# A hybrid decoder trunk: the low halves off the diagonal given to GpSimd, and the mask of the maxima added within VectorE's maximum

## The chip, the cores and the metric

The kernel runs on one core of a Trainium2 chip. The metric is the device time of one execution in microseconds (us). The core has five engines that take their instructions in order, each from its own queue: TensorE (PE, matrix products into PSUM banks), VectorE (DVE), ScalarE (ACT), GpSimd (POOL) and SyncE (SP, which issues most DMAs).

## The reference, cut to what matters

A sequence of 2048 tokens passes a Mamba-2 mixer and then a layer of multi-head latent attention with 16 heads; the change is in the attention alone. Its core is

```
for i in range(S // Q_BLOCK):
    q0 = i * Q_BLOCK
    kv_len = q0 + Q_BLOCK
    s = einsum('bqhd,bkhd->bhqk', q_nope[:, q0:kv_len], k_nope[:, :kv_len]) + \
        einsum('bqhr,bkr->bhqk', q_rope[:, q0:kv_len], k_rope[:, :kv_len])
    mask = (q0 + local)[:, None] >= arange(kv_len)[None, :]
    p = softmax(where(mask, s * scale, -inf))
    outs.append(einsum('bhqk,bkhd->bqhd', p, v[:, :kv_len]))
```

A query and a key have 96 elements in a head (64 and 32 rotary ones), a value 64. The results are wanted close to float32, so the kernel holds operands as pairs of float16 numbers, a high half and a low half, and multiplies the pairs.

## The kernel before, in words

The layers before the attention take about the first 2000 us of the program, the attention the next 800, and the output projection with the last norm (`back`) the rest. In the attention a **job** is one head with one quarter of the queries (512, four blocks of 128): 64 jobs, head by head, quarter by quarter. Each job does two things.

**Maxima** (`maxima`, L1224). For each block of 128 queries, TensorE forms the scores against all its keys with queries on the partitions, high halves only (L1236), in chunks of at most 1024 keys, one or two a block. Where a chunk ends on the diagonal, a further product adds the 128x128 mask (L1238). VectorE takes the maximum of each row of the chunk (L1239). When the last chunk of a job is done, some small VectorE instructions make the four columns of maxima into two float16 rows: `m` (L1244, where blocks had two chunks), `me` (L1248), the cast into `nm` (L1250), its low half (L1251), and a transpose `rT` (L1253). SyncE writes `rT` to HBM (L1254) and reads it back as rows 96 and 97 of the job's queries (L1257), so that the score product subtracts the maximum by itself.

**Scores and values.** The keys of a job are taken two blocks at a time, a **duo**. `scores` (L1260) forms the transposed scores, keys on the partitions, by three products for each block (L1269 to L1271) and a mask on the diagonal (L1273). ScalarE takes the exponential into `x` (L1276) and its high half into `PTs` (L1278). The **low** half, `x` less the high half, is two instructions: the first 512 columns on VectorE (L1279), the rest on GpSimd (L1280). Off the diagonal a duo has 1024 columns; the two on the diagonal have 896 and 384. `values` (L1283) then multiplies each 128 columns with V by three products (L1296 to L1298), the third with the low half. `finish` (L1305) divides the sums (L1310, L1313, tiles `ri` and `Op`), and for every second head `store` (L1318) transposes two heads' results.

The order on TensorE is written out by hand (L1342 to L1357): at each **step** first the chunks of maxima that are due (at most 1024 columns a step, at latest four steps ahead of the job's first duo), then a waiting store, then the scores of one duo, then the values of the duo that came HELD steps before. The other engines' order is the scheduler's, fixed when the program is built. The PSUM banks `s` are three for chunks, scores and stores together, so TensorE waits until VectorE or ScalarE has read an earlier one.

A head has 20 steps. They are counted here from 0 in each head: steps 0 and 1 are the first quarter (both on the diagonal), 2 to 5 the second, 6 to 11 the third, 12 to 19 the fourth; the last two of each quarter are on the diagonal. The maxima of the fourth quarter end with a 1024 chunk at step 8, and its first scores are at step 12. Chunk, maximum, scores, values and low are named by the step or duo, as in "low 7".

Of the kernel before, what the change touches and what calls it, by code (L numbers as in the profile page):

```python
# [37 lines left out]
SZ = 4  # L38
EV0 = ['big', 'Xp', 'big', 'Sp', 'wsp']
EV1 = ['big', 'yT', 'Xp', 'big', 'Sp']  # L40
HELD = 2
READY = 4
TURN = 2
MSCALE = 64.0
# [22 lines left out]
class Net:  # L67
# [1124 lines left out]
    def heads(self, sp):  # L1192
# [3 lines left out]
        for u in turned:  # L1196
            nc.gpsimd.memset(u, 0.0)

        def cuts(kv):

            first = kv if kv <= 2 * TB else TB if kv <= 3 * TB else 2 * TB
            return [(0, first)] + ([(first, kv - first)] if kv > first else [])
# [21 lines left out]
        def maxima(n, j, i, c0, w, last):  # L1224

            h, qb = jobs[n]
            if (j, i) == (0, 0):
                peak[n] = self.t(sp, "mx", [P, 4, 2], bufs=3)
                if n + 2 < len(jobs):
                    self.load_q(*jobs[n + 2])  # L1230
            Q, K, qs = quer[h, qb], keys[h % 2], slice(j * P, (j + 1) * P)
            s = bank().rearrange("p a b -> p (a b)")
            for at in range(0, w, TB):
                c = min(TB, w - at)
                diag = last and at + c == w
                mm(s[:, at:at + c], Q[0:96, 0, qs], K[0:96, 0, c0 + at:c0 + at + c], start=True, stop=not diag)  # L1236
                if diag:
                    mm(s[:, w - P:w], self.idb, self.mk, start=False, stop=True)  # L1238
            v.tensor_reduce(peak[n][:, j, i:i + 1], s[:, :w], AX.X, ALU.max)  # L1239
            if last and j == 3:  # L1240
                m = peak.pop(n)
                if i:
                    x = self.t(sp, "m", [P, 4], bufs=2)
                    v.tensor_tensor(x, m[:, :, 0], m[:, :, 1], ALU.max)  # L1244
                else:
                    x = m[:, :, 0]
                e = self.t(sp, "me", [P, 4], bufs=2)
                v.tensor_scalar(e, x, -1.0 / MSCALE, LN16 / MSCALE, ALU.mult, ALU.add)  # L1248
                u = turned[n % 2]
                v.tensor_copy(u[:, 0:4], e)  # L1250
                v.tensor_tensor(u[:, 4:8], e, u[:, 0:4], ALU.subtract)  # L1251
                r = self.t(sp, "rT", [P, 32], F16, bufs=2)
                v.transpose(r, u)  # L1253
                nc.sync.dma_start(self.m_d[n], r)  # L1254
                rows = self.m_d[n].rearrange("(g r) q -> r g q", r=32)
                for k in range(2):
                    nc.sync.dma_start(quer[h, qb][96 + k:97 + k, 0, :].rearrange("p (j g q) -> p j g q", j=4, q=32),  # L1257
                                      rows[4 * k:4 * k + 4].unsqueeze(0))

        def scores(n, kb):  # L1260

            h, qb = jobs[n]
            Q, K, s = quer[h, qb], keys[h % 2], bank()
            ja, jb = max(kb - 4 * qb, 0), max(kb + 1 - 4 * qb, 0)
            at, end = ja * P, 2 * TB - jb * P
            for b, j in enumerate((ja, jb)):
                ks, c = slice((kb + b) * P, (kb + b + 1) * P), slice(j * P, TB)
                o = s[:, 1, 0:TB - j * P] if b else s[:, 0, c]
                mm(o, K[0:98, 0, ks], Q[0:98, 0, c], start=True, stop=False)  # L1269
                mm(o, K[0:96, 0, ks], Q[0:96, 1, c], start=False, stop=False)  # L1270
                mm(o, K[0:96, 1, ks], Q[0:96, 0, c], start=False, stop=kb < 4 * qb)  # L1271
                if kb >= 4 * qb:
                    mm(o[:, 0:P], self.mk, self.idb, start=False, stop=True)  # L1273
            s = s.rearrange("p a b -> p (a b)")[:, at:end]
            x = self.t(sp, "x", [P, 2 * TB], bufs=3)
            act(x[:, at:end], s, AF.Exp)  # L1276
            u = self.t(sp, "PTs", [P, 2, 2 * TB], F16, bufs=HELD + 2)
            act(u[:, 0, at:end], x[:, at:end], AF.Copy)  # L1278
            v.tensor_tensor(u[:, 1, at:TB], x[:, at:TB], u[:, 0, at:TB], ALU.subtract)  # L1279
            nc.gpsimd.tensor_tensor(u[:, 1, TB:end], x[:, TB:end], u[:, 0, TB:end], ALU.subtract)  # L1280
            return u

        def values(n, kb, u):  # L1283

# [44 lines left out]
                with self.tc.issue_after(done.ins):  # L1329
                    self.load_wo(qb)  # L1330

        step, later, held, made = [0], [], [], 0
        self.load_k(1, 0, NB)
        self.load_v(1)

        def waiting():
            for at, f in list(later):
                if at <= step[0]:
                    later.remove((at, f))
                    f()  # L1340

        for i, (n, kb) in enumerate(duos):  # L1342
            step[0] = i
            while cols[made] < due[i]:
                maxima(*chunks[made])
                made += 1
            waiting()
            held.append((n, kb, scores(n, kb)))
            if len(held) > HELD:
                values(*held.pop(0))  # L1350
        while held:
            step[0] += 1
            values(*held.pop(0))
            waiting()
# [201 lines left out]
```

## Time and profile before

| | us |
|---|---|
| median of 3 runs | 2988.53 (2984.73 to 2989.96) |
| the profiled execution, its own time | 2990.72 |
| its span in the profile | 2988.5 |
| TensorE busy in the span | 2869.4 (96%) |
| VectorE busy | 2255.6 (75%) |
| ScalarE busy | 1795.1 (60%) |
| GpSimd busy | 807.5 (27%) |

The profile is one execution as the hardware profiler recorded it, with starts counted from the span's start. L12 is a line of the kernel. A row of a group gives line, engine, operation, the tiles it writes and reads, shapes and count, then the busy time, the mean of one in ns, and the idle time of the engine just before with what ended it. In a timeline a row gives start and length in us. In the list of waits a row gives who waited for whom, with us in total, times and the longest. Records of TensorE overlap, since a product starts while the one before it drains.

### The profile page before, as it was taken

How to read it: one execution, taken by the hardware profiler on the slowest of the kernel's cores; microseconds unless marked ns; L12 is line 12 of the kernel's file. 1: busy time of each engine (PE TensorE's matmuls, PEld its weight loads, DVE VectorE, ACT ScalarE, POOL GpSimd, SP SyncE). 2: the span in 40 equal slices, each digit the busy share in tenths (PEclk: the TensorE clock that was granted, in tenths of full speed). 3: DMA queues.
4: the chain of work that ended last, by engine and by line, in shares of the span. 5: the costliest groups of instructions: out<-in, count | busy, mean ns of one | idle time of the engine just before them, and what ended most of it. 6: DMA issues, size and time to landing. Idle time of an engine off the chain costs nothing.

```text
span 2988.5 us, 58345 instructions
## 1 busy us (share of the span) xinstructions
PE 2869.4 (96%) x21838; PEld 1689.2 (57%) x21838; DVE 2255.6 (75%) x4570; ACT 1795.1 (60%) x3592; POOL 807.5 (27%) x862
## 2 busy tenths in 40 slices
PE   7899999999999999999999999999999999998998
PEld 3456556555555554554554554546666666665787
DVE  6789987787877878788766435358989999989454
ACT  8777656665766656556553433327777777777422
POOL 0212122121221212222212112215454445455300
PEclk9999999999999999999999999999999999999999
DMA  8765435544464446545447655641222121222452
GB/s 286 242 216 176 165 122 194 172 155 141 154 228 158 139 169 201 186 157 191 136 130 249 197 171 177 193 154 44 54 57 65 49 62 46 70 65 75 151 203 106
DMA packets 244751, 441.28 MB, mean 148 GB/s; under 512 B 69842, under 2 KB 111506, under 8 KB 243028
## 3 DMA queue, kind: packets, MB, share of 16 engines
q1 hardware_dynamic: 233332, 401.64, 42.0%
q0 software_dynamic: 11136, 35.92, 3.3%
q8 instruction: 171, 2.80, 0.4%
q14 instruction: 112, 0.92, 0.1%
HBM read 332.73 MB, written 104.73 MB: 146 GB/s over the span
## 4 chain that ended last, share of the span: by engine, by line
PE 33%; DVE 10%; ACT 5%; issue 3%; DMA 1%; POOL 1%; SPq 0%; DVEq 0%; ACTq 0%; POOLq 0%
DVE PTs L1279 4%; PE mm L83 4%; PE mm L84 4%; PE mm L85 4%; DVE mx L1239 3%; PE tr L83 3%; PE tr L84 3%; PE tr L85 3%; PE s L1269 2%; PE s L1270 2%; PE s L1271 2%; ACT x L1276 2%; ACT PTs L1278 2%; PE s L1236 2%; PE o L1298 1%
## 5 line engine op out<-in xcount | busy, mean ns | idle before, releaser
L1280 POOL TENSOR_TENSOR PTs<-x,PTs 128x512 f16<-128x512 f32 (+1 forms) x320 | 381.0, 1193 | 397.4 <-ACT PTs L1278 195.0
L1276 ACT ACTIVATE x<-s 128x1024 f32<-128x1024 f32 (+1 forms) x320 | 285.1, 891 | 190.3 <-PE s L1271 105.0
L1239 DVE TENSOR_REDUCE mx<-s 128x1 f32<-128x1024 f32 (+7 forms) x384 | 339.5, 900 | 30.7 <-PE s L1238 19.3
L1279 DVE TENSOR_TENSOR PTs<-x,PTs 128x512 f16<-128x512 f32 x320 | 291.5, 922 | 46.0 <-ACT PTs L1278 21.2
L83 PE MATMUL mm<-xT,wsp 128*128 128x512 f16 x800 | 306.5, 383 | 8.1 <-ACT wsp L114 6.3
L84 PE MATMUL mm<-xT,wsp 128*128 128x512 f16 x800 | 305.8, 382 | 0.0
L85 PE MATMUL mm<-xT,wsp 128*128 128x512 f16 x800 | 304.8, 381 | 0.0
L1278 ACT ACTIVATE PTs<-x 128x1024 f16<-128x1024 f32 (+1 forms) x320 | 296.9, 928 | 9.9
L1269 PE MATMUL s<-xT,K 98*128 98x512 f16 (+3 forms) x640 | 223.3, 349 | 25.7 <-DVE mx L1239 17.7
L1298 PE MATMUL o<-K,PTs 128*128 128x65 f16 x2176 | 235.2, 193 | 11.4 <-DVE PTs L1279 7.2
L1297 PE MATMUL o<-K,PTs 128*128 128x65 f16 x2176 | 236.3, 194 | 0.0
L1296 PE MATMUL o<-K,PTs 128*128 128x64 f16 x2176 | 236.0, 192 | 0.0
L83 PE MATMUL mm<-wsp,xT 128*128 128x512 f16 (+1 forms) x640 | 231.1, 362 | 3.9 <-ACT craw L605 3.7
L84 PE MATMUL mm<-wsp,xT 128*128 128x512 f16 (+1 forms) x640 | 231.2, 362 | 3.2 <-DVE wsp L115 3.2
L611 DVE SCALAR_TENSOR_TENSOR cacc<-craw,pack,cacc 128x512 f32<-128x512 f32 x288 | 214.6, 773 | 24.0 <-ACT cacc L609 23.0
L85 PE MATMUL mm<-wsp,xT 128*128 128x512 f16 (+1 forms) x640 | 231.1, 361 | 0.0
L801 POOL TENSOR_TENSOR Xp<-Xw,Xp 128x512 fp32r<-128x512 f32 x64 | 89.5, 1399 | 501.0 <-ACT Xp L800 301.2
L1270 PE MATMUL s<-xT,K 96*128 96x512 f16 (+3 forms) x640 | 223.7, 350 | 0.0
L1271 PE MATMUL s<-xT,K 96*128 96x512 f16 (+3 forms) x640 | 222.4, 348 | 0.0
L1296 PEld LDWEIGHTS <-PTs 128*128 128x128 f16 x2176 | 203.1, 97 | 27.5 <-issue 0.4
L1297 PEld LDWEIGHTS <-PTs 128*128 128x128 f16 x2176 | 201.6, 97 | 23.1 <-issue 0.3
L1298 PEld LDWEIGHTS <-PTs 128*128 128x128 f16 x2176 | 200.5, 98 | 15.3 <-DVE PTs L1279 8.5
(459 smaller groups left out, 7178.2 us busy)
## 6 DMA issues: line engine op xcount, KB each, us to landing
wsp<-wi_d SPq DMA_DIRECT2D x96, 512.0 KB
big<-cumT SPq DMA_DIRECT2D x64, 512.0 KB
wraw<-in_ssm_w_out_dram SPq DMA_DIRECT2D x96, 256.0 KB
wi_d<-wsp SPq DMA_DIRECT2D x32, 512.0 KB
wsp<-wo_d SPq DMA_DIRECT2D x32, 512.0 KB
wsp<-wu_d SPq DMA_DIRECT2D x28, 512.0 KB
hx<-in_ssm_w_in_dram SPq DMA_DIRECT2D x48, 256.0 KB
wraw<-in_ssm_w_in_dram SPq DMA_DIRECT2D x48, 256.0 KB
```

Of the source, the lines that this page charges most:

```text
L83: mm(out, l_hi, r_hi, start=start, stop=False)
L84: mm(out, l_hi, r_lo, start=False, stop=False)
L85: mm(out, l_lo, r_hi, start=False, stop=stop)
L1239: v.tensor_reduce(peak[n][:, j, i:i + 1], s[:, :w], AX.X, ALU.max)
L1270: mm(o, K[0:96, 0, ks], Q[0:96, 1, c], start=False, stop=False)
L1276: act(x[:, at:end], s, AF.Exp)
L1278: act(u[:, 0, at:end], x[:, at:end], AF.Copy)
L1279: v.tensor_tensor(u[:, 1, at:TB], x[:, at:TB], u[:, 0, at:TB], ALU.subtract)
L1280: nc.gpsimd.tensor_tensor(u[:, 1, TB:end], x[:, TB:end], u[:, 0, TB:end], ALU.subtract)
L1296: mm(o[:, 0:64], hi, V[:, k, 0:64], start=k == 0 and j == 0, stop=False, skip_group_check=True)
L1297: mm(o[:, 0:65], hi, V[:, k, 64:129], start=False, stop=False, skip_group_check=True)
L1298: mm(o[:, 0:65], lo, V[:, k, 64:129], start=False, stop=k == 4 * qb + j, skip_group_check=True)
```

## The change

The diff, with unchanged lines left out:

```
-HELD = 2
+HELD = 3
...
+        fence = self.t(sp, "fence", [P, 2 * TB], BF16, bufs=1)
+        nc.gpsimd.memset(fence[:, :2 * TB - P], 0.0)
+        nc.gpsimd.tensor_copy(fence[:, 2 * TB - P:], self.mk)
...
             for at in range(0, w, TB):
                 c = min(TB, w - at)
-                diag = last and at + c == w
-                mm(s[:, at:at + c], Q[0:96, 0, qs], K[0:96, 0, c0 + at:c0 + at + c], start=True, stop=not diag)
-                if diag:
-                    mm(s[:, w - P:w], self.idb, self.mk, start=False, stop=True)
-            v.tensor_reduce(peak[n][:, j, i:i + 1], s[:, :w], AX.X, ALU.max)
+                mm(s[:, at:at + c], Q[0:96, 0, qs], K[0:96, 0, c0 + at:c0 + at + c], start=True, stop=True)
+            if last:
+                junk = self.t(sp, "junk", [P, 2 * TB], BF16, bufs=1)
+                v.tensor_tensor_reduce(junk[:, :w], s[:, :w], fence[:, 2 * TB - w:], 1.0, -3.0e38, ALU.add, ALU.max,
+                                       accum_out=peak[n][:, j, i:i + 1])
+            else:
+                v.tensor_reduce(peak[n][:, j, i:i + 1], s[:, :w], AX.X, ALU.max)
...
-            v.tensor_tensor(u[:, 1, at:TB], x[:, at:TB], u[:, 0, at:TB], ALU.subtract)
-            nc.gpsimd.tensor_tensor(u[:, 1, TB:end], x[:, TB:end], u[:, 0, TB:end], ALU.subtract)
+            if kb < 4 * qb:
+                lows(u, x, at, end, nc.gpsimd)
+            else:
+                fresh.append((u, x, at, end, v))
             return u
+
+        def lows(u, x, at, end, engine):
+
+            engine.tensor_tensor(u[:, 1, at:end], x[:, at:end], u[:, 0, at:end], ALU.subtract)
...
             waiting()
+            if fresh:
+                lows(*fresh.pop())
             held.append((n, kb, scores(n, kb)))
             if len(held) > HELD:
                 values(*held.pop(0))
+        lows(*fresh.pop())
```

Four things happen. The low half of a duo off the diagonal is one GpSimd instruction of 1024 columns (192 of them) instead of two of 512 on two engines. The low half of a duo on the diagonal is one VectorE instruction of 896 or 384 columns (64 of each), written in the program one step later, behind that step's maxima. The 256 maxima whose chunk ends on the diagonal add a row of zeros and the mask, the tile `fence`, within the instruction that takes the maximum; each is two VectorE instructions, the sum with the maximum and the reading of the accumulator, and 256 mask products of TensorE go. And values follow three steps behind the scores instead of two.

The changed lines move the scheduler's order on VectorE. The first place is steps 8 to 12 of the ninth head: the maxima `mx` of steps 7 and 8, the small instructions that end the fourth quarter's maxima (`m` to `rT`), and the lows (`PTs<-x`). Before, from the maximum of step 8 to the one behind low 11:

```order
L1239 TENSOR_REDUCE mx_28854<-s_29128 128x1
L1279 TENSOR_TENSOR PTs_29111<-x_29109,PTs_29111 128x512
L1244 TENSOR_TENSOR m_29133<-mx_28854 128x4
L1248 TENSOR_SCALAR me_29135<-m_29133 128x4
L1250 CAST nm_4004_21664<-me_29135 128x4
L1251 TENSOR_TENSOR nm_4004_21664<-me_29135,nm_4004_21664 128x4
L1253 STREAM_TRANSPOSE rT_29139<-nm_4004_21664 128x32
L1279 TENSOR_TENSOR PTs_29153<-x_29151,PTs_29153 128x512
L1279 TENSOR_TENSOR PTs_29191<-x_29189,PTs_29191 128x512
L1279 TENSOR_TENSOR PTs_29230<-x_29228,PTs_29230 128x512
L1239 TENSOR_REDUCE mx_29297<-s_29302 128x1
L1279 TENSOR_TENSOR PTs_29269<-x_29267,PTs_29269 128x256
```

And now, from the same maximum to low 11; L1242 is the masked maximum with its reading, L1250 to L1259 are `m` to `rT`, L1322 and L1325 a finish, L1293 a low:

```order
L1242 ISA junk_28953,mx_28674<-s_28950,fence_21667 128x1024
L1242 ISA mx_28674 128x1
L1250 TENSOR_TENSOR m_28955<-mx_28674 128x4
L1254 TENSOR_SCALAR me_28957<-m_28955 128x4
L1256 CAST nm_4004_21664<-me_28957 128x4
L1322 RECIPROCAL ri_28987<-o_28846 128x4
L1257 TENSOR_TENSOR nm_4004_21664<-me_28957,nm_4004_21664 128x4
L1325 TENSOR_TENSOR Op_28989<-o_28846,ri_28987 128x4x64
L1259 STREAM_TRANSPOSE rT_28961<-nm_4004_21664 128x32
L1293 TENSOR_TENSOR PTs_29039<-x_29037,PTs_29039 128x896
L1242 ISA junk_29110,mx_29103<-s_29108,fence_21667 128x128
L1293 TENSOR_TENSOR PTs_29077<-x_29075,PTs_29077 128x384
```

Low 7 no longer stands ahead of `m`, nor lows 8 and 9 behind `rT`; a finish has come in between the cast and the transpose; lows 10 and 11 stand around the first maximum of step 12 as they did, longer than before. (The reading behind L1242 of step 12 lies between the last two rows.)

The second place is steps 0 to 2 of the same head on VectorE, from the last maximum of step 0, which ends the third quarter's maxima. Before:

```order
L1239 TENSOR_REDUCE mx_28618<-s_28802 128x1
L1244 TENSOR_TENSOR m_28807<-mx_28618 128x4
L1248 TENSOR_SCALAR me_28809<-m_28807 128x4
L1250 CAST nm_4003_21663<-me_28809 128x4
L1251 TENSOR_TENSOR nm_4003_21663<-me_28809,nm_4003_21663 128x4
L1253 STREAM_TRANSPOSE rT_28813<-nm_4003_21663 128x32
L1239 TENSOR_REDUCE mx_28854<-s_28859 128x1
L1279 TENSOR_TENSOR PTs_28829<-x_28827,PTs_28829 128x512
L1279 TENSOR_TENSOR PTs_28874<-x_28872,PTs_28874 128x256
L1310 RECIPROCAL ri_28887<-o_28534 128x4
L1239 TENSOR_REDUCE mx_28854<-s_28893 128x1
```

And now:

```order
L1242 ISA junk_28623,mx_28433<-s_28620,fence_21667 128x1024
L1242 ISA mx_28433 128x1
L1293 TENSOR_TENSOR PTs_28591<-x_28589,PTs_28591 128x384
L1250 TENSOR_TENSOR m_28625<-mx_28433 128x4
L1254 TENSOR_SCALAR me_28627<-m_28625 128x4
L1256 CAST nm_4003_21663<-me_28627 128x4
L1257 TENSOR_TENSOR nm_4003_21663<-me_28627,nm_4003_21663 128x4
L1245 TENSOR_REDUCE mx_28674<-s_28679 128x1
L1259 STREAM_TRANSPOSE rT_28631<-nm_4003_21663 128x32
L1293 TENSOR_TENSOR PTs_28648<-x_28646,PTs_28648 128x896
L1242 ISA junk_28721,mx_28674<-s_28718,fence_21667 128x640
```

The low of the last diagonal duo (384) now stands behind the last maximum of step 0 and not ahead of the step; the low of step 0's duo (896) stands ahead of the maximum of step 2 as before, and that of step 1's duo has moved behind it.

More of the change, by code (lines that the diff above doesn't have):

```diff
@@ L1330, in store @@
                     self.load_wo(qb)
-        step, later, held, made = [0], [], [], 0
+        step, later, held, fresh, made = [0], [], [], [], 0
         self.load_k(1, 0, NB)
```

## The prediction, made before the changed kernel was run

> **What bounds the kernel now.** I read the page first, then the busy time by stretches, the waits, the groups by shape, and one head of the attention in order of time. The change touches only the attention, so the stretches come first; a row gives its length, then busy time and instructions of TensorE, its weight loads, VectorE, ScalarE and GpSimd.
>
> ```profile
> 2200.00:2400.00 200.00, 190.88 (x2536) 126.12 (x2535) 182.22 (x288) 152.44 (x175) 98.68 (x85) 1.00 0.22 55
> 2400.00:2600.00 200.00, 190.11 (x2513) 125.14 (x2512) 182.94 (x294) 150.39 (x173) 96.90 (x83) 1.00 0.23 60
> ```
>
> TensorE shows 95% busy, VectorE 91%, ScalarE 76%, GpSimd 49%, at the full granted clock (1.00). Busy time overstates TensorE, because records overlap. How far apart its products start, and how long a head lasts, stands in the timeline (start, length, idle before in brackets):
>
> ```profile
> 2380.31 0.38 PE L1269 MATMUL s<-xT,K 98*128 98x512 f16 x1 [0.72 <-DVE mx L1239]
> 2419.28 0.38 PE L1269 MATMUL s<-xT,K 98*128 98x512 f16 x1
> 2419.50 0.38 PE L1270 MATMUL s<-xT,K 96*128 96x512 f16 x1
> 2425.78 0.19 PE L1296 MATMUL o<-K,PTs 128*128 128x64 f16 x1
> 2425.87 0.19 PE L1296 MATMUL o<-K,PTs 128*128 128x64 f16 x1
> 2426.57 0.22 PE L1238 MATMUL s<-mk,idb 128*128 128x128 bf16 x1
> 2426.63 0.27 PE L1236 MATMUL s<-K,xT 96*128 96x256 f16 x1
> 2427.39 0.22 PE L1238 MATMUL s<-mk,idb 128*128 128x128 bf16 x1
> 2428.69 0.38 PE L1269 MATMUL s<-xT,K 98*128 98x512 f16 x1 [1.08 <-DMA xT<-m_d]
> 2443.13 0.22 PE L1238 MATMUL s<-mk,idb 128*128 128x128 bf16 x1
> 2444.30 0.38 PE L1236 MATMUL s<-K,xT 96*128 96x512 f16 x1 [0.95 <-DVE mx L1239]
> ```
>
> A 512-column product takes 0.217 us of the queue, three small value products 0.09, a mask 0.06. A head has 17408 columns of scores (34 times 512), so 102 x 0.217 = 22.1 us of scores, 7.4 of maxima, 408 x 0.03 = 12.2 of values, 32 x 0.06 = 1.9 of masks, 0.4 of transposes: 44 us. From step 12 of one head (2380.31) to the next (2428.69) are 48.4. So TensorE waits 4.3 us a head, and an idle row hides 0.16 more (0.38 of record less 0.217). Two of the waits are above, at steps 12 and 17: 1.3 and 1.2 us between starts, less the 0.06. What TensorE waits for:
>
> ```profile
> PE s L1269 <- DVE mx L1239: 17.7, 35, 1.7
> PE s L1236 <- DVE mx L1239: 7.2, 10, 1.0
> PE o L1298 <- DVE PTs L1279: 7.2, 11, 2.3
> ```
>
> So TensorE bounds the attention, and VectorE being late with the maxima, whose banks must come free, is what it waits for.
>
> **The change, part by part.**
>
> *Masks of the maxima.* 256 products of 0.06 us go: 0.96 us a head. Seven of the sixteen stand just ahead of the two waits below (steps 0, 2, 8 and the four of 12); there TensorE only waits longer. Nine count: -0.5 us a head.
>
> *Masked maximum.* The groups of VectorE, with mean ns of one:
>
> ```profile
> L1279 DVE TENSOR_TENSOR PTs<-x,PTs 128x512 f16<-128x512 f32 x256 | 250.5, 979 | 44.2 <-ACT PTs L1278 20.5 <-POOL PTs L1280 17.3 <-PE o L1298 5.7
> L1239 DVE TENSOR_REDUCE mx<-s 128x1 f32<-128x1024 f32 x111 | 134.3, 1210 | 6.9 <-PE s L1236 5.6 <-PE s L1238 0.3
> L1239 DVE TENSOR_REDUCE mx<-s 128x1 f32<-128x512 f32 x77 | 51.9, 673 | 4.7 <-PE s L1236 4.6
> L1313 DVE TENSOR_TENSOR Op<-o,ri 128x256 f32<-128x256 f32 x64 | 26.9, 421 | 1.6
> L1239 DVE TENSOR_REDUCE mx<-s 128x1 f32<-128x256 f32 x15 | 6.2, 411 | 0.0
> L884 ACT ACTIVATION_READ_ACCUMULATOR yt<-y 128x1 f32 x64 | 12.0, 187 | 0.0
> ```
>
> No such sum with a maximum runs before. Its nearest row is L1313, one input in PSUM and one in SBUF: 421 ns for 256, against 411 for the plain maximum, so the main part costs the same. It issues a second instruction that reads the accumulator: from 0 (hidden in the overlap of neighbours) to 187 ns (ScalarE's row). I take 0.1, as VectorE's rows overlap by about that. In all 26 us, inside the stretches below.
>
> *Low halves.* VectorE's 256 lows of 512 and 64 of 256 leave; 64 of 896 and 64 of 384 come. At 1.05 ns an element ((1210 - 673) / 512) and from an undisturbed 0.69 for 512, they take 1.09 and 0.56: 106 us. GpSimd's time comes from its undisturbed rows, and what it does to VectorE from the stretch around the maximum of step 8, now:
>
> ```profile
> 2403.55 0.91 POOL L1280 TENSOR_TENSOR PTs<-x,PTs 128x384 f16<-128x384 f32 x1 [2.74 <-DVE nm L1250]
> 2422.43 1.16 POOL L1280 TENSOR_TENSOR PTs<-x,PTs 128x512 f16<-128x512 f32 x1 [0.40 <-ACT PTs L1278]
> 2420.35 1.67 POOL L1280 TENSOR_TENSOR PTs<-x,PTs 128x512 f16<-128x512 f32 x1 [0.70 <-DVE mx L1239]
> 2402.86 0.16 DVE L1244 TENSOR_TENSOR m<-mx 128x4 f32<-128x4 f32 x1
> 2419.11 1.21 DVE L1239 TENSOR_REDUCE mx<-s 128x1 f32<-128x1024 f32 x1
> 2420.32 0.69 DVE L1279 TENSOR_TENSOR PTs<-x,PTs 128x512 f16<-128x512 f32 x1
> 2420.93 1.11 DVE L1244 TENSOR_TENSOR m<-mx 128x4 f32<-128x4 f32 x1
> 2422.08 0.17 DVE L1248 TENSOR_SCALAR me<-m 128x4 f32<-128x4 f32 x1
> 2422.49 1.11 DVE L1251 TENSOR_TENSOR nm<-me,nm 128x4 f16<-128x4 f32 x1
> 2423.64 0.21 DVE L1253 STREAM_TRANSPOSE rT<-nm 128x32 f16<-128x32 f16 x1
> ```
>
> (1.16 - 0.91) / 128 is 1.95 ns an element, so 1024 take 2.16 us; 192 of them are 415 us of some 785, and GpSimd is not the bound. But m and nm, four elements wide, take 1.11 us where GpSimd is at work and 0.16 where not: a VectorE instruction with two inputs in SBUF waits until GpSimd's has ended. GpSimd's are now twice as long.
>
> The Trainium skill speaks against this part: "GPSIMD Engine Reference", Engine selection, puts two-input elementwise work on VectorE, GpSimd being about twice as slow. The rows say 1.16 against 0.69 (1.7 times); twice VectorE's 1.23 for 1024 would be an estimate of 2.5, which would add 0.3 to each blocked instruction below.
>
> *Entry.* The first maximum now needs the fence, which GpSimd writes last:
>
> ```profile
> 1999.47 0.28 DVE L1239 TENSOR_REDUCE mx<-s 128x1 f32<-128x128 f32 x1
> 1999.85 0.68 POOL L1103 DMA_DIRECT2D qn_d<-Xp  x1 [1.27 <-DVE mx L1239]
> 2000.41 0.31 POOL L1197 MEMSET nm<- 128x32 f16 x2
> ```
>
> GpSimd is free at 2000.7; a memset of 896 and a copy of 128 cost between 0.3 (two like the memsets here) and 1.8 us (896 elements at the two-input rate). I take 0.8, near the middle: the maximum starts at 2001.5, +2 us, once; queued behind it are all later maxima, and the first scores wait for them.
>
> *Step 17 and step 11.* No VectorE low is left between the maxima there: the wait at 2444.30 goes, -1.1 us a head. The maximum of step 16 now stands behind nm of step 15, which GpSimd may hold up for most of 2 us: +0.3.
>
> *Steps 0 to 3.* From the maximum of step -1 to the one of step 2 VectorE now does 896, 512, 1024 and 1024, 640 of maxima, and lows of 1.09, 0.56, 1.09 with m to rT (0.9) between: 1.09 + 0.67 + 1.21 + 1.21 + 0.81 + 2.74 + 0.9 + 0.3 (reads) = 8.9 us, in one piece. TensorE needs from that chunk to the scores of step 3, by the spacings above, 3.8 for scores, 2.4 for values and 1.8 for chunks: 8.0. Scores 3 take the bank of step 2's chunk, so they wait 0.9 to 1.2, and two ScalarE waits behind them may add 0.3. Now it waits in these steps, the second only in heads that store:
>
> ```profile
> 2402.88 0.27 PE L1269 MATMUL s<-xT,K 98*128 98x256 f16 x1 [0.37 <-DVE mx L1239]
> 2407.43 0.41 PE L1323 MATMUL s<-pack,Op 128*128 128x128 f32 x2 [0.60 <-DVE Op L1313]
> ```
>
> With 0.16 hidden in each, 0.5 to 1.3, and I take +0.2.
>
> *Steps 8 to 12, which decide.* With HELD 3 TensorE does the values of duo 4 (21 products, 0.63 us) ahead of chunk 8, not those of duo 5 (0.27), so chunk, maximum and scores of step 8 come 0.37 later against duo 7, less the mask's 0.06. Low 7 stays where it is on GpSimd, 2420.35. Maximum 8 ends at 2420.45, just behind, so m waits to 2420.35 + 2.16 = 2422.5 (now 2422.04). me, the cast and the reciprocal of a finish that now stands ahead of nm bring nm to 2423.1; low 8 has started at 2422.43 + 0.37 = 2422.8 and holds it to 2424.96. Then Op (0.42, now ahead of the transpose) and rT: 2425.6, against 2423.85. From there the row's way through HBM takes 2428.69 - 2423.85 = 4.84 us, so the scores of step 12 start at 2430.4, not at 2428.69 as here, where the row came last, nor near 2428.35, as in heads where VectorE's maxima did (the row at 2380.31): +1.7 to +2.05. What VectorE does itself meets it there:
>
> ```profile
> 2425.17 0.95 ACT L1278 ACTIVATE PTs<-x 128x896 f16<-128x896 f32 x1
> 2427.87 1.47 DVE L1239 TENSOR_REDUCE mx<-s 128x1 f32<-128x256 f32 x3
> ```
>
> Low 10 waits for this copy (2426.5 then) and for GpSimd's low 9 (to 2427.1); low 10, a 128 maximum, low 11 and the 256 maximum, whose bank scores 12 takes, need 1.09 + 0.4 + 0.56 + 0.5: 2429.65, against 2427.87 + 0.41 = 2428.3 now. So +1.3 even if m slipped in first. I take +2.0.
>
> *Sum.* -0.5 - 1.1 + 0.3 + 0.2 + 2.0 = +0.9 us a head; some 15 heads are in this rhythm: +13, and +2 at the entry. The profiled execution took 2990.7 (span 2988.5), so 3006; the median of the runs shown lies 2.2 lower: 3003.
>
> **The rivals.**
>
> *Relief.* VectorE has 190 lows fewer, and TensorE's waits are for VectorE. If low 7 starts after m, and lows 10 and 11 are done when chunk 12 comes, the waits at 12 and 17 go (1.1 each) and all masks count: 16 x (2.2 + 0.96) = 51, less the entry's 2 and the 0.2 and 0.3 a head: about 2948. For it: GpSimd's start beats m by 0.1 us only. Against it: low 10 and low 9 by the rows above.
>
> *The stretches cancel.* m slips in first, lows 10 and 11 do not: -0.5 - 1.1 + 0.5 + 1.3 = +0.2 a head, +3, and the entry: 2994, no change that can be told.
>
> *A dear masked maximum.* Each 0.3 us longer (from 0.1 on it costs; half the rate would be 0.5 to 1): three stand in steps 0 to 3 and three in the way to scores 12, 6 x 0.3 x 16 = +29 on the forecast, 3032. It would also do so by waiting for GpSimd. Against it: L1313 keeps 421 ns. [...]
>
> **How the numbers follow.** A measurement of this kernel tells some 0.2% (6 us) from no change. Forecast 0.46, since m's 0.1 us and the order of lows 10 and 11 are two separate reasons; relief 0.24; cancelling 0.20; dear maximum 0.10. Slower is 0.56, same 0.20, faster 0.24. The range leaves out the lower half of relief and the upper half of the dear maximum: 2948 to 3035. The forecast's own range is 2995 to 3015 (m and low 10 between their ends).
>
> **What would show it.** Right: L1238 gone; GpSimd's lows at 2.1 to 2.3 us; m and nm at step 8 held for 2 us each; scores 12 idle 2 to 4 us in every head, by the row or by VectorE; no wait at step 17; head period 49.3. Wrong: the masked maximum of 1024 above 1.4 us with its read, m at 0.16 in step 8, or a head period under 48.

## The result, and the profile after

| | before | changed |
|---|---|---|
| median, us | 2986.89 (4 runs, 2984.73 to 2989.96) | 3110.91 (4 runs, 3107.97 to 3113.17) |
| the profiled execution, us | 2990.72 | 3112.48 |
| its span, us | 2988.5 | 3110.7 |

The ratio is 1.0414, 95% interval 1.0396 to 1.0432. The change costs 124 us where 16 were forecast. The first scores of the attention start at 2009.45 us (2009.66 before), and 195 us lie behind its last scores (196 before), so all of it lies inside the attention. The busy time by stretches of the changed kernel, with the columns of the prediction's rows (length, then TensorE, its weight loads, VectorE, ScalarE and GpSimd, the granted clock of TensorE, the DMA share, GB/s):

```profile
2200.00:2400.00 200.00, 171.06 (x2064) 108.01 (x2061) 145.77 (x261) 129.75 (x147) 93.24 (x44) 0.90 0.17 44
2400.00:2600.00 200.00, 177.71 (x2163) 113.63 (x2162) 147.49 (x262) 133.64 (x154) 89.32 (x43) 0.90 0.21 54
```

VectorE fell from 182 busy of 200 to 146, for the most part because the same work is spread over longer heads: with the lengths of a head below, it is busy for 44 us of a head before and for 41 now. TensorE fell from 190 to 174, and the granted clock from 1.00 to 0.90. No engine is full, so look for waits. This is VectorE's timeline in the eighth head, from the end of the maximum of step 8 to the transpose, then GpSimd's lows at the same time, then TensorE (start, length, engine and line, idle before in brackets):

```profile
2423.37 1.23 DVE L1242 CUSTOM_DVE_ANT_0 junk<-s,fence 128x1024 bf16<-128x1024 f32 x1 [1.15 <-PE s L1239]
2424.64 2.05 DVE L1250 TENSOR_TENSOR m<-mx 128x4 f32<-128x4 f32 x1
2426.72 0.17 DVE L1254 TENSOR_SCALAR me<-m 128x4 f32<-128x4 f32 x1
2426.93 2.14 DVE L1256 CAST nm<-me 128x4 f16<-128x4 f32 x1
2429.10 2.04 DVE L1257 TENSOR_TENSOR nm<-me,nm 128x4 f16<-128x4 f32 x1
2431.06 0.41 DVE L1325 TENSOR_TENSOR Op<-o,ri 128x256 f32<-128x256 f32 x1
2431.39 0.20 DVE L1259 STREAM_TRANSPOSE rT<-nm 128x32 f16<-128x32 f16 x1
2424.54 2.13 POOL L1293 TENSOR_TENSOR PTs<-x,PTs 128x1024 f16<-128x1024 f32 x1 [0.33 <-ACT PTs L1284]
2426.92 4.20 POOL L1293 TENSOR_TENSOR PTs<-x,PTs 128x1024 f16<-128x1024 f32 x2 [0.25 <-DVE me L1254]
2431.62 1.09 PE L1335 MATMUL s<-pack,Op 128*128 128x128 f32 x4 [4.67 <-DVE rT L1259]
2432.50 0.63 PE L1275 MATMUL s<-xT,K 98*128 98x512 f16 x1
2432.93 0.63 PE L1276 MATMUL s<-xT,K 96*128 96x512 f16 x1
```

Put the ends beside each other. `m` ends at 2426.69, where GpSimd's first low ends (2426.67). The cast ends at 2429.07 and `nm` at 2431.14; GpSimd's two lows from 2426.92 to 2431.12, in one record, have their boundary near 2429.02. Three instructions of four elements each wait for one whole GpSimd low: behind `m` the next low starts just ahead of the cast, and the third low follows the second without a gap, ahead of `nm`. Before, this stretch from the end of the maximum to the transpose took 3.5 us (2420.32 to 2423.85); now it takes 7.0 (2424.60 to 2431.59). The other heads from the second to the fourteenth show the same two figures.

Who is late by that? Here it is not the row of the maxima but the store: its four transposes on TensorE need `Op`, and `Op` stands behind `nm` on VectorE. TensorE sits idle for 4.67 us. Then comes the second price: the products behind the wait start 0.43 us apart (2432.50, 2432.93), twice the 0.217 of the undisturbed ones, and their records last 0.63 instead of 0.38. That is the granted clock at half, as the profile gives it (last but two in the row):

```profile
2429.10:2435.90 6.80, 4.28 (x30) 2.92 (x31) 2.49 (x4) 1.24 (x2) 2.02 (x1) 0.50 0.02 4
```

Only every second head has a store at step 10. In the others (the ninth here) the row of the maxima is the late one: TensorE waits for a maximum's bank and then, ahead of the scores of step 12, for the row to come back from HBM.

```profile
2491.00 0.59 PE L1239 MATMUL s<-K,xT 96*128 96x512 f16 x1 [1.51 <-DVE mx L1242]
2494.08 0.58 PE L1275 MATMUL s<-xT,K 98*128 98x512 f16 x1 [2.49 <-DMA xT<-m_d]
```

At step 15 of the eighth head cast and `nm` are held again, where the maxima of the next head's second quarter end:

```profile
2448.11 2.10 DVE L1256 CAST nm<-me 128x4 f16<-128x4 f32 x1
2450.25 2.05 DVE L1257 TENSOR_TENSOR nm<-me,nm 128x4 f16<-128x4 f32 x1
2452.47 0.65 DVE L1245 TENSOR_REDUCE mx<-s 128x1 f32<-128x512 f32 x1
2453.17 1.12 PE L1239 MATMUL s<-K,xT 96*128 96x512 f16 x3 [1.96 <-DVE mx L1245]
```

The maximum at 2452.47 stands behind both, and TensorE waits for its bank. The groups of VectorE and of GpSimd over the attention, and the three largest rows of what TensorE's products wait for (us in total, times, longest):

```profile
L1256 DVE CAST nm<-me 128x4 f16<-128x4 f32 x62 | 70.5, 1137 | 2.0
L1257 DVE TENSOR_TENSOR nm<-me,nm 128x4 f16<-128x4 f32 x62 | 66.7, 1076 | 1.5
L1250 DVE TENSOR_TENSOR m<-mx 128x4 f32<-128x4 f32 x32 | 35.6, 1112 | 0.5
L1242 DVE CUSTOM_DVE_ANT_0 junk<-s,fence 128x1024 bf16<-128x1024 f32 x47 | 57.2, 1217 | 18.4 <-PE s L1239 18.4
L1242 DVE DVE_READ_ACCUMULATOR2_ANT mx<- 128x1 f32 x246 | 20.1, 82 | 0.0
L1293 POOL TENSOR_TENSOR PTs<-x,PTs 128x1024 f16<-128x1024 f32 x192 | 407.1, 2128 | 484.0 <-ACT PTs L1284 282.2 <-PE s L1277 130.9 <-issue 49.8
```

```profile
PE s L1335 <- DVE rT L1259: 37.3, 8, 4.7
PE s L1239 <- DVE mx L1245: 28.5, 14, 2.1
PE s L1239 <- DVE mx L1242: 22.3, 16, 8.5
```

`m`, cast and `nm` take 1.1 us in the mean. The masked maximum costs what a plain one does. The first row of the waits is new; the one before, where TensorE waited for `Op`, came to 4.1 us.

Where the time went by step, from the starts of the first score product of each step, mean of ten heads, us:

| steps | 0-8 | 9-10 | 11-12 | 13-15 | 16-17 | 18-19 | head |
|---|---|---|---|---|---|---|---|
| before | 20.63 | 4.26 | 6.10 | 7.02 | 5.85 | 4.48 | 48.35 |
| changed | 19.16 | 7.66 | 8.66 | 6.86 | 9.06 | 4.84 | 56.24 |

More than half of the head became no slower, and steps 0 to 8 are 1.5 us faster. Steps 9 to 12 lost 6.0 and steps 16 and 17 lost 3.2. The mean of steps 9 to 12 hides two cases. In the heads with that store (called odd below, since the kernel counts heads from 0) steps 9 and 10 lost 7.3 and steps 11 and 12 gained 0.4; in the even ones steps 9 and 10 gained 0.5 and steps 11 and 12 lost 5.5.

A second account splits TensorE's time by the distance between starts of neighbouring products, from 2014 us to the end of the attention. An excess of 0.5 to 1.3 times the usual distance counts as half speed, any other of at least 0.15 us as a wait. Before there were 65 us of waits and 4 at half speed, now 139 and 70. So the growth of the stretch by 124 us is 74 of waits and 66 of half speed, less 14 for the masks and some 2 of small remainders. Nearly half of the loss is not waiting at all, but running slowly behind a wait.

### The profile page after: what moved, and what is told of

The parts are those of the page before. It is cut to its first block, busy times and chain, and to the rows that moved or that the text cites. A ratio compares the mean times of both kernels' runs of the same rounds, so it can differ in the third digit from the quotient of the medians.

```text
span 3110.7 us, 57237 instructions
## 1 busy us (share of the span) xinstructions
PE 2910.9 (94%) x21582; PEld 1697.6 (55%) x21582; DVE 2212.5 (71%) x4634; ACT 1798.2 (58%) x3592; POOL 833.6 (27%) x736
## 4 chain that ended last, share of the span: by engine, by line
PE 57%; DVE 22%; issue 9%; DMA 5%; ACT 5%; POOL 1%; SPq 1%; POOLq 0%; DVEq 0%; ACTq 0%
PE mm L83 10%; PE mm L84 10%; PE mm L85 10%; DVE cacc L611 3%; DVE junk L1242 3%; PE s L1275 3%; PE tr L84 3%; PE s L1239 3%; PE tr L83 3%; PE tr L85 3%; PE s L1276 3%; PE s L1277 3%; DVE nm L1256 2%; PE tr L878 2%; PE o L1310 1%
## 5 line engine op out<-in xcount | busy, mean ns | idle before, releaser
L1293 POOL TENSOR_TENSOR PTs<-x,PTs 128x1024 f16<-128x1024 f32 x192 | 407.1, 2128 | 484.0 <-ACT PTs L1284 282.2
L1282 ACT ACTIVATE x<-s 128x1024 f32<-128x1024 f32 (+1 forms) x320 | 284.9, 890 | 276.0 <-PE s L1277 185.4
L1242 DVE CUSTOM_DVE_ANT_0 junk<-s,fence 128x768 bf16<-128x768 f32 (+7 forms) x256 | 226.9, 886 | 138.7 <-PE s L1239 129.5
L1275 PE MATMUL s<-xT,K 98*128 98x512 f16 (+3 forms) x640 | 238.7, 373 | 30.5 <-DMA xT<-m_d 15.1
L1310 PE MATMUL o<-K,PTs 128*128 128x65 f16 x2176 | 244.4, 197 | 6.1 <-POOL PTs L1293 6.0
L1308 PE MATMUL o<-K,PTs 128*128 128x64 f16 x2176 | 245.4, 197 | 0.0
L1309 PE MATMUL o<-K,PTs 128*128 128x65 f16 x2176 | 245.2, 198 | 0.0
L1276 PE MATMUL s<-xT,K 96*128 96x512 f16 (+3 forms) x640 | 238.8, 373 | 0.0
L1239 PE MATMUL s<-K,xT 96*128 96x512 f16 (+3 forms) x640 | 181.8, 373 | 59.1 <-DVE mx L1245 28.5
L1277 PE MATMUL s<-xT,K 96*128 96x512 f16 (+3 forms) x640 | 236.0, 369 | 0.0
L1308 PEld LDWEIGHTS <-PTs 128*128 128x128 f16 x2176 | 210.8, 100 | 30.6 <-issue 6.1
L1309 PEld LDWEIGHTS <-PTs 128*128 128x128 f16 x2176 | 209.1, 100 | 25.5 <-issue 4.7
L1310 PEld LDWEIGHTS <-PTs 128*128 128x128 f16 x2176 | 208.3, 101 | 6.8 <-POOL PTs L1293 6.6
```

What stands on the lines that cost most here:

```text
L1242: v.tensor_tensor_reduce(junk[:, :w], s[:, :w], fence[:, 2 * TB - w:], 1.0, -3.0e38, ALU.add, ALU.max, accum_out=peak[n][:, j, i:i + 1])
L1293: engine.tensor_tensor(u[:, 1, at:end], x[:, at:end], u[:, 0, at:end], ALU.subtract)
L1308: mm(o[:, 0:64], hi, V[:, k, 0:64], start=k == 0 and j == 0, stop=False, skip_group_check=True)
L1309: mm(o[:, 0:65], hi, V[:, k, 64:129], start=False, stop=False, skip_group_check=True)
L1310: mm(o[:, 0:65], lo, V[:, k, 64:129], start=False, stop=k == 4 * qb + j, skip_group_check=True)
```

## The experiments

Theory A at the start was that GpSimd's lows of 1024 hold the small VectorE operations. Its rivals were the masked maximum (B), HELD = 3 (C), and lows that simply come too late (D). The first four kernels ran on one chip, where the kernel before took 2991.26 us. Ratios are to the kernel before, with the 95% interval. The kernel before took 2986.89 to 2992.05 us in the sets of this document, so a difference in us between kernels of two sets is good to some 5 us.

**1. The masked maximum alone.** The kernel before, with `fence` and

```
-                if diag:
-                    mm(s[:, w - P:w], self.idb, self.mk, start=False, stop=True)
-            v.tensor_reduce(peak[n][:, j, i:i + 1], s[:, :w], AX.X, ALU.max)
+            if last:
+                v.tensor_tensor_reduce(junk[:, :w], s[:, :w], fence[:, 2 * TB - w:], ...)
```

> The kernel before, with the masked maximum alone: the mask is added within VectorE's maximum, and the low halves and HELD stay as before (VectorE and GpSimd 512 each, HELD = 2). Theory A (the loss comes from GpSimd's lows of 1024, which hold each of the small VectorE operations m, cast and nm for a whole low): this half costs nothing, TensorE loses 256 products of 0.06 us and VectorE gains some 0.1 us for each read of the accumulator, so 2970 to 2992 us, granted clock of the attention 1.00. Theory B (the masked maximum and its accumulator read are what delays the banks and the maxima's rows): most of the 124 us shows here, 3050 us or more.

Measured 2986.72 us, 0.998 (0.9971 to 0.9989). This half of the change is a small gain: 47.77 us a head in place of 48.35, most of it at steps 16 and 17 (5.25 in place of 5.85). B falls.

**2. The lows alone.** The changed kernel with the diff of the maxima undone:

```
+                if diag:
+                    mm(s[:, w - P:w], self.idb, self.mk, start=False, stop=True)
-            if last:
-                v.tensor_tensor_reduce(junk[:, :w], s[:, :w], fence[:, 2 * TB - w:], ...)
-            else:
-                v.tensor_reduce(peak[n][:, j, i:i + 1], s[:, :w], AX.X, ALU.max)
+            v.tensor_reduce(peak[n][:, j, i:i + 1], s[:, :w], AX.X, ALU.max)
```

> The changed kernel, but the mask is again a TensorE product and the maximum a plain one; the low halves stay all on GpSimd off the diagonal, with HELD = 3. Theory A (GpSimd's lows of 1024 hold m, cast and nm for 2 us each): all of the loss is here, 3095 to 3130 us, with m, cast and nm at 1.0 us or more in the mean and the granted clock of the attention near 0.9. Theory B (the masked maximum): 2990 to 3030 us.

Measured 3059.1 us, 1.0233 (1.0206 to 1.026). Some 68 of the 124 us are here, which lies between the two expectations. `m` and `nm` are held as in the changed kernel (1112 and 1085 ns), the cast only half as often (635):

```profile
L1251 DVE TENSOR_TENSOR nm<-me,nm 128x4 f16<-128x4 f32 x62 | 67.3, 1085 | 1.5
L1250 DVE CAST nm<-me 128x4 f16<-128x4 f32 x62 | 39.4, 635 | 2.0
L1244 DVE TENSOR_TENSOR m<-mx 128x4 f32<-128x4 f32 x31 | 34.5, 1112 | 0.5
```

A few tenths of a microsecond in the order of chunk, maximum and low decide whether an operation slips in between two lows. So the two halves do not add up: the masked maximum, a gain by itself, moves the cast into the next low.

**3. HELD = 2 in the changed kernel.**

```
-HELD = 3
+HELD = 2
```

> The changed kernel with HELD = 2 instead of 3, everything else as changed. Theory A (GpSimd's lows of 1024 hold m, cast and nm): those three are held just the same, the time stays above 3080 us. Theory C (holding the values of three duos, which puts the chunk, the maximum and the finish later against GpSimd's lows, is what costs): back to 2990 to 3030 us. A also allows it to be slower than 3111 us, since with HELD = 2 the values of a duo come one step sooner after a low of 2.1 us.

Measured 3029.09 us, 1.0123 (1.0105 to 1.0141). That misses A's number, and is what C expected. The groups say why:

```profile
L1256 DVE CAST nm<-me 128x4 f16<-128x4 f32 x62 | 40.9, 660 | 2.1
L1257 DVE TENSOR_TENSOR nm<-me,nm 128x4 f16<-128x4 f32 x62 | 27.3, 441 | 2.1
L1250 DVE TENSOR_TENSOR m<-mx 128x4 f32<-128x4 f32 x32 | 7.0, 219 | 0.5
```

`m` is held once in 32 times. With HELD = 2 it mostly reaches VectorE just as one low ends, ahead of the next. So HELD either costs by itself (C), or only by its phase against GpSimd (A, mended). Experiment 10 tells these apart.

**4. Each GpSimd low in two instructions of 512.**

```
-                lows(u, x, at, end, nc.gpsimd)
+                lows(u, x, at, TB, nc.gpsimd)
+                lows(u, x, TB, end, nc.gpsimd)
```

> The changed kernel with each GpSimd low of 1024 issued as two instructions of 512, so that GpSimd does the same work (some 0.1 to 0.3 us more a duo) but ends an instruction twice as often. Theory A (a small VectorE operation waits for the GpSimd instruction that is running to end): m, cast and nm fall from 1.1 us in the mean to 0.5 to 0.7, the row of the maxima and Op come some 3 us sooner in each head, and the time falls to 3000 to 3050 us, with the granted clock of the attention back near 1.0. Theory D (GpSimd simply delivers the lows too late, or its memory traffic slows VectorE at large): unchanged or worse, 3105 us or more.

Measured 3005.1 us, 1.0043 (1.0031 to 1.0055). GpSimd does the same work and is busier (337 us of the 600 from 2100 to 2700, against 271, partly because the heads are shorter), and yet some 110 of the 124 us are gone, because it lets go twice as often: `m` 600, cast 415, `nm` 562 ns. D falls.

The next four ran on another chip (before 2990.65 us).

**5. Three of the small operations in a form with one input.** `m` and the cast become reductions, `nm` a reduction over a value and its negated high part, which costs one more tensor_scalar.

```
-                    v.tensor_tensor(x, m[:, :, 0], m[:, :, 1], ALU.max)
+                    v.tensor_reduce(x, m, AX.X, ALU.max)
...
-                v.tensor_copy(u[:, 0:4], e)
-                v.tensor_tensor(u[:, 4:8], e, u[:, 0:4], ALU.subtract)
+                v.tensor_reduce(u[:, 0:4], e[:, :, 0:1], AX.X, ALU.max)
+                v.tensor_scalar(e[:, :, 1], u[:, 0:4], -1.0, 0.0, ALU.mult, ALU.add)
+                v.tensor_reduce(u[:, 4:8], e, AX.X, ALU.add)
```

> The changed kernel, with GpSimd's lows of 1024 and HELD = 3 kept, but the small operations of a job in forms with one input each: m and the cast as reductions over a last axis of 2 and of 1, nm as a reduction that adds e and the negated high part, which one more tensor_scalar writes (one VectorE instruction more a job). Theory A (GpSimd's running instruction holds only VectorE operations that share its memory port, the two-input ones and the cast): m, cast and nm fall to 0.15 to 0.3 us each, the row of the maxima and Op come some 6 us sooner in each head, the stalls of 7 to 8 us at steps 9 and 11 and of 5 us at step 16 go, granted clock 0.98 or more, 2945 to 2985 us. Theory D (any small VectorE operation is held, or the lows themselves come too late): 3080 us or more. If the tensor_scalar that negates is held as well, it lies between, near 3000 us.

Measured 3012.15 us, 1.0065 (1.0047 to 1.0083), the middle case. Its groups are the clearest rows of the study:

```profile
L1257 DVE TENSOR_SCALAR me<-nm 128x4 f32<-128x4 f16 x62 | 56.1, 904 | 1.6
L1254 DVE TENSOR_SCALAR me<-m 128x4 f32<-128x4 f32 x32 | 32.8, 1024 | 1.0
L1256 DVE TENSOR_REDUCE nm<-me 128x4 f16<-128x4 f32 x62 | 9.7, 156 | 2.0
L1259 DVE TENSOR_REDUCE nm<-me 128x4 f16<-128x8 f32 x62 | 9.6, 155 | 1.1
L1250 DVE TENSOR_REDUCE m<-mx 128x4 f32<-128x8 f32 x32 | 5.0, 157 | 0.5
```

The reductions run through GpSimd's lows as if these weren't there. The tensor_scalar at L1254, one input and never long before (228 and 276 ns in the changed kernel), now takes the place of the held operation: it had only been lucky to stand behind one.

By the Trainium skill, "SBUF — State Buffer", Who interferes with whom, copy, cast and tensor_scalar can enter modes that use the ports shared with GpSimd, and a reduction never contends on this chip. These rows agree: 904 and 1024 ns beside 155 to 157.

**6. The waits filled with useless products.** In odd heads 16 products of 512 columns go ahead of the second quarter's store, in even heads 12 ahead of the first scores of the fourth quarter, into banks that the next product overwrites (224 products in all).

```
+        def fill(o, h, qb, count):
+            for i in range(count):
+                mm(o, keys[h % 2][0:96, 1, 0:P], quer[h, qb][0:96, 1, :], start=True, stop=True)
...
+            if qb == 1:
+                fill(ps, h, 3, 16)
```

> The changed kernel with useless TensorE work added where it waits longest: in each odd head 16 products of 512 columns (3.5 us) ahead of the store's transposes of the second quarter, in each even head 12 (2.6 us) ahead of the first scores of the fourth quarter, into banks that the next product overwrites; the waits there last 4.8 and 2.8 us, so the products fit into them. Theory A with the clock (the granted clock drops to half behind a long wait, and the 70 us of products at half speed are a consequence of the waits): added work makes it faster, 3070 to 3100 us, the products behind the filled waits 0.217 us apart again and not 0.43. Rival E (the half speed does not come from the idle time): 3105 us or more, products behind the waits still 0.43 us apart.

Measured 3097.09 us, 1.0355 (1.0338 to 1.0371), so 14 us less than the changed kernel (18 by the ratios), with 49 us of products more (224 x 0.217). TensorE's timeline in an odd head; L1269 are the added products, L1344 the store, L1282 and L1283 scores:

```profile
2420.49 3.62 PE L1269 MATMUL s<-xT,K 96*128 96x512 f16 x16
2425.24 0.66 PE L1344 MATMUL s<-pack,Op 128*128 128x128 f32 x4 [1.13 <-DVE Op L1332]
2425.73 0.38 PE L1282 MATMUL s<-xT,K 98*128 98x512 f16 x1
2425.95 0.38 PE L1283 MATMUL s<-xT,K 96*128 96x512 f16 x1
```

The wait is still there for the store, but TensorE worked through most of it, and the scores behind start 0.22 us apart. Half speed over the attention fell from 70 to 47 us. In odd heads it went as expected. In even heads the wait is spread over three places of 0.6 to 1.7 us ahead of the added products, which there ran mostly at half speed themselves. E falls: the slow clock is a consequence of the waits.

**7. The store two steps later.**

```
-TURN = 2
+TURN = 4
```

> The changed kernel with TURN = 4: the store of a finished pair is put on TensorE two steps later, so that its transposes no longer wait for Op, which stands on VectorE behind cast and nm. Theory A (part of the loss is the store waiting for Op in odd heads): the wait of 4.8 us ahead of the transposes goes, the odd heads come down from 58.2 us toward the even heads' 54.4 or less, 3065 to 3095 us. Rival F (the store only waits in the place where the row of the maxima would hold TensorE anyway): the odd heads then wait at step 11 like the even ones, unchanged within 10 us, 3100 to 3120 us.

Measured 3063.22 us, 1.0243 (1.0227 to 1.0258). Odd heads fall from 57.56 to 51.72 us, even ones stay (54.92 to 55.29). Steps 9 and 10 come down to 4.02, below before; steps 11 and 12 rise from 8.66 to 10.11, where the row is now the late one. So taking the store's wait away was worth 48 us, and F, that it merely stood in another's place, accounts for a third: in odd heads steps 9 and 10 fall by 7.3 us and steps 11 and 12 rise by 2.4.

**8. The masked maximum alone, with the reductions of experiment 5.** The kernel of experiment 1, and `m`, cast and `nm` as there:

```
-                    v.tensor_tensor(x, m[:, :, 0], m[:, :, 1], ALU.max)
+                    v.tensor_reduce(x, m, AX.X, ALU.max)
...
```

> The kernel before with the masked maximum alone (lows and HELD as before), and the small operations in the same one-input forms. Theory A: m falls from 0.60 and nm from 0.36 us in the mean to 0.15 to 0.3, rows come up to 1 us sooner where they are the last that scores 12 wait for: 2970 to 2986 us, a little under the 2987 of the masked maximum alone. If TensorE waits there for VectorE's maxima and not for the row: the same as the masked maximum alone, 2983 to 2992 us.

Measured 2986.17 us, 0.9983 (0.9973 to 0.9992), not to be told from experiment 1. With lows of 512 the row is not what scores 12 wait for.

The third chip (before 2991.41 us).

**9. All four small operations as reductions.** The sign comes from the reduction; the scale by 64 goes, so the keys' last rows hold 1; the offset becomes the bias of Exp. The result that is computed stays the same.

```
+                v.tensor_reduce(e[:, :, 0], m[:, :, 0:i + 1], AX.X, ALU.max)
+                v.tensor_reduce(u[:, 0:4], e[:, :, 0:1], AX.X, ALU.max, negate=True)
+                v.tensor_reduce(e[:, :, 1], u[:, 0:4].unsqueeze(2), AX.X, ALU.max)
+                v.tensor_reduce(u[:, 4:8], e, AX.X, ALU.add, negate=True)
...
-            act(x[:, at:end], s, AF.Exp)
+            act(x[:, at:end], s, AF.Exp, bias=ln16)
```

> The changed kernel with GpSimd's lows of 1024 and HELD = 3 kept, and all four small operations of a job as reductions with one input: the scale of the row goes (the keys' last rows hold 1 and not 64, the sign comes from the reduction, the offset LN16 from the bias of Exp), so that no tensor_scalar, cast or two-input operation is left in the chain from the last maximum to the transpose. Theory A (what GpSimd holds is the form of these operations, and this is where the 124 us come from): all four take 0.15 to 0.17 us, the stalls at steps 9, 11 and 16 shrink to 2 us or less, granted clock 0.98 or more, 2950 to 2985 us, so at or below the kernel before, with all of GpSimd's doubled lows in place. Theory D (the lows of 1024 are late for the values, or load the memory): 3005 us or more as with two reductions of four.

Measured 2982.1 us, 0.9971 (0.9961 to 0.9982): all of the loss is gone, with GpSimd's lows of 1024 and HELD = 3 in place. The groups, then the busy time by stretches:

```profile
L1256 DVE TENSOR_REDUCE nm<-me 128x4 f16<-128x8 f32 x62 | 10.0, 161 | 1.5
L1254 DVE TENSOR_REDUCE me<-nm 128x4 f32<-128x4 f16 x62 | 9.7, 157 | 2.0
L1251 DVE TENSOR_REDUCE me<-mx 128x4 f32<-128x8 f32 (+1 forms) x62 | 9.7, 157 | 1.5
L1253 DVE TENSOR_REDUCE nm<-me 128x4 f16<-128x4 f32 x62 | 9.7, 157 | 2.0
```

```profile
2200.00:2400.00 200.00, 191.73 (x2502) 124.08 (x2500) 135.44 (x317) 159.79 (x176) 106.32 (x51) 0.98 0.22 58
2400.00:2600.00 200.00, 191.72 (x2471) 123.65 (x2470) 136.49 (x322) 161.22 (x178) 105.19 (x50) 0.98 0.24 60
```

TensorE is busy for 192 of 200 us again at a clock of 0.98, and VectorE only for 136. In the ninth head the transpose of the fourth quarter's row now ends 1.2 us behind the maximum (2416.71 to 2417.95), where it was 7.0; the other heads from the second to the fourteenth show the same. Experiment 8, with three of the operations rewritten and lows of 512, gained nothing, so it is not the rewriting alone that pays here.

**10. The same with HELD = 2.**

> The same with HELD = 2. If HELD = 3 costs by itself (theory C), this is faster than with HELD = 3. By theory A HELD = 3 costs only by where it puts the small operations against the lows; with nothing left to hold, HELD = 2 brings back the waits of the values for the lows of 2.1 us (28 us of them in the changed kernel with HELD = 2), so 10 to 30 us slower than with HELD = 3.

Measured 3007.76 us, 1.0056 (1.0038 to 1.0075). With nothing left to hold, HELD = 2 is the slower of the two by 26 us, and TensorE waits 37.8 us for GpSimd's lows at the values. So C falls as well: HELD = 3 cost the changed kernel time only by where it put `m` and `nm` against the lows.

**11. Experiment 9 with TURN = 4.**

> The same with HELD = 3 and TURN = 4 (the store two steps later). By theory A Op is no longer late, so the store waits for nothing at TURN = 2 either: within 8 us of TURN = 2. If the store still waits for Op: 8 to 25 us faster.

Measured 2999.61 us, 1.0028 (1.0018 to 1.0039): 17.5 us slower than experiment 9, where both expectations had it equal or faster. Steps 11 and 12 take 9.11 us in place of 8.08, and half speed is 42 us in place of 31. Why a later store does this was not tried.

The last one ran on a fourth chip (before 2992.05 us).

**12. Experiment 9 with VectorE's lows one step later.** Aimed at the 8.1 us that steps 11 and 12 still take.

```
-                fresh.append((u, x, at, end, v))
+                fresh.append((step[0] + 2, (u, x, at, end, v)))
...
-            if fresh:
-                lows(*fresh.pop())
+            if fresh and fresh[0][0] <= i:
+                lows(*fresh.pop(0)[1])
```

> The kernel with all small operations as reductions (2982.1 us), and VectorE's lows on the diagonal one step later, behind the maxima of the step after next. There VectorE still waits 5 us for ScalarE's copy of step 10 with a finished chunk's maximum queued behind it, and TensorE waits 2.6 us for that maximum's bank, with the products behind it 0.43 us apart. By theory A this is what is left of the loss: without it the steps 11 and 12 fall from 8.7 us to 5 to 6 and the granted clock rises to 1.00, 2935 to 2965 us. Rival: the row of the maxima, or the values waiting for a low that is now later, takes the place of this wait: 2975 to 2995 us.

Measured 2977.82 us, 0.9954 (0.9938 to 0.997). The interval overlaps that of experiment 9, so the two are not told apart, and steps 11 and 12 stay at 8.23 us. But the edit did not do what it was meant to. The order on VectorE is the scheduler's, and in the trace it is that of experiment 9 throughout the attention; the low of step 10 still stands ahead of the first maximum of step 12 and waits for ScalarE's copy:

```profile
2424.75 1.30 DVE L1292 TENSOR_TENSOR PTs<-x,PTs 128x896 f16<-128x896 f32 x1 [5.03 <-ACT PTs L1283]
2425.97 0.28 DVE L1244 CUSTOM_DVE_ANT_0 junk<-s,fence 128x128 bf16<-128x128 f32 x1
```

So this run is a second measurement of experiment 9's order, and whether the wait is the lows' was not tested. What TensorE's chunks wait for is in equal parts VectorE's maximum and ScalarE's Exp:

```profile
PE s L1241 <- DVE mx L1244: 11.7, 15, 2.1
PE s L1241 <- ACT x L1281: 11.5, 14, 0.9
```

Both readers have to free one of the three banks. Which of them would have to be sooner, and whether moving the lows would do it, stays open.

## Why the prediction was wrong

*Right.* The masked maximum: 1217 ns for 1024 and 82 for its read, against 1.2 and 0.1 forecast. The masks: a small gain. GpSimd's lows: 2128 ns against 2.16 us. The mechanism of steps 8 to 12: a small operation waits until GpSimd's low has ended, and in even heads the row of step 12 comes late by it. The direction followed from it. That the low starts 0.1 us ahead of `m` came out too (2424.54 and 2424.64), by luck: the prediction's own terms, 2420.32, 0.31 later and 0.1 for the read, put the end of maximum 8 at 2420.7 and not at 2420.45.

*The step that failed: "me, the cast and the reciprocal of a finish ... bring nm to 2423.1".* The cast was taken as free: the prediction had an instruction with two inputs in SBUF wait, and the cast, with one, took 0.17 us before.

```profile
2422.28 0.17 DVE L1250 CAST nm<-me 128x4 f16<-128x4 f32 x1
```

Both were too little. The cast is one of the held forms (1137 ns in the mean), and in this row it merely stood in the gap between two lows, one ended at 2422.02 and the next started at 2422.43. With the cast held, `nm` meets not the second low but the third, so the chain of step 8 is three lows, 6.2 us, and not two. The page of the Trainium skill cited at experiment 5, "SBUF — State Buffer", Who interferes with whom, names the cast beside the instructions with two inputs, and the cast's row in the changed kernel sides with it.

*A waiter left out.* `Op` was counted as 0.42 us ahead of `rT`, but not followed to its reader. The store needs it, and TensorE takes its instructions in order: 37.3 us of waits in eight heads, 48 us by experiment 7. The +2.0 for steps 8 to 12 came out as +6.0 over steps 9 to 12 in the mean: 7.3 at the store in odd heads, 5.5 at the row in even ones, less what the other two steps gained.

*A sign.* For steps 16 and 17 the prediction summed -1.1 (no low left between the maxima) and +0.3 (`nm` of step 15 may hold the maximum of step 16). The gain is there, but smaller: with nothing held (experiment 9) the two steps take 5.45 us in place of 5.85. But cast and `nm` of step 15 take 2.10 and 2.05 us one after the other, where 0.3 was set down, and the two steps lost 3.2.

*A term left out.* Waits were priced at their length. Behind them the clock fell to half, which added 66 us to 74 of waits. The eleven waits of 1.0 to 1.2 us before had no such price; the three of 1.9 to 2.6 us had, and the prediction did not look behind them.

*Steps 0 to 3* were forecast at +0.2 and the entry at +2; the steps came out at -0.7 (steps 0 to 8 at -1.5) and the entry at nothing.

*The rivals.* Relief, 2948, was right in that VectorE's lows were a burden: with nothing held, steps 0 to 8 gain 1.6 us a head. Even then steps 11 and 12 give 2.0 back, and the best version (2982.1, and 2977.8 for the same order in experiment 12) stands well above it. No rival held a third operation, the store or the clock, so the range ended at 3035.

## What to carry to other kernels

When GpSimd's instructions get longer, list every small VectorE instruction that may wait for one of them, by its form and not by the time that it took before: a short row may only be luck. In a chain of small operations each one can wait for a whole GpSimd instruction of its own, so either rewrite the chain in forms that are not held (reductions, here) or cut GpSimd's instructions shorter. Follow each late result to its reader on an in-order engine, and add some 2 us to each wait of TensorE of 2 us or more: in the changed kernel 31 such waits, 103 us, came with 66 us more at half speed. Before reading the time of an edit that is to move an instruction, look in the trace whether it has moved (experiment 12).

## What the runs showed of the hardware

- A four-element VectorE instruction takes 0.16 us as a reduction and up to 2.15 us as a cast, a tensor_scalar or a two-input operation, when a GpSimd subtraction of 1024 elements (2.13 us) is running.
- The half clock comes behind short waits. In the changed kernel 35 of the 40 waits of 1.0 us or more were followed, within 8 us, by 1.4 to 3.2 us of loss at half speed, those of 2.1 to 2.9 us mostly among them (six waits of 1.7 us stand just ahead of one of 2.7 to 2.9 us and share its loss). Before, none of eleven waits of 1.0 to 1.2 us was, and all three of 1.9 to 2.6 us were. In and behind the wait of 4.67 us shown above, the granted clock was 0.50 from 2429.1 to 2435.9. The Trainium skill, "TensorE: Matmul & The Clock Gate", HAM oscillation — how this bites in real kernels, gives the rule that idle gaps should stay under some 3.4 us; here shorter ones cost the clock as well.
- More work on TensorE can shorten the program: 49 us of useless products in its waits took 14 to 18 us off.
